# Three 256-column matmuls per group and one VectorE product in the channel-major projections of a two-layer decoder trunk

## The chip, the core and the metric

The kernel runs on one core of one Trainium2 chip. The metric is the device time of one execution in microseconds (us); less is better. A measurement of this kernel is given as the median of its runs. Engines are named as the profile names them: PE is the TensorE matmul, PEld its weight load (which overlaps PE), DVE is VectorE, ACT is ScalarE, POOL is GpSimd, SP is SyncE.

## The reference, cut to what matters

The reference is a causal decoder trunk of two layers over 256 tokens of width 2048 in float32. Each layer normalises its input, multiplies it by wide input weights, mixes over the tokens, projects back and adds the residual; then comes a gated feed-forward part with a causal convolution of width 3 over the tokens.

```python
def rmsnorm(x, g):
    y = xf * lax.rsqrt(jnp.mean(xf * xf, axis=-1, keepdims=True) + NORM_EPS)
    return y * g
...
proj = xn @ w_in                 # even layer: q, k, v, o, gates, u, z
...
def conv_ffn(xn, w_up, conv_w, conv_b, w_down):
    h = xn @ w_up                # 2048 -> 11264
    h = causal_depthwise_conv(h, conv_w) + conv_b
    a, b = jnp.split(h, 2, axis=-1)
    return (jax.nn.silu(a) * b) @ w_down
...
for layer in range(DEPTH):
    h = h + mixer(rmsnorm(h, mix_norm[layer]), ...)
    h = h + conv_ffn(rmsnorm(h, ffn_norm[layer]), ...)
```

The part of the rmsnorm that is one number per token (the reciprocal root) commutes with the matmul, so the kernel applies it to the product. That number is called the token factor here.

## The kernel before, in words

All matmuls run on values that are split in two: hi is the float32 value rounded to the matmul's own float32r type, lo is the rest. A product of two split values is the sum of three matmuls, hi by hi, hi by lo and lo by hi. The activations lie channel-major in four tiles `xc0` to `xc3`, each `[128, 4, 2, 256]`: 128 channels on the partitions, 4 k-tiles, the hi part and the lo part, and 256 tokens. The hi and the lo part of a k-tile stand side by side, 512 columns.

There are two kinds of projection.

- **Token-major** (`tok_plan` with `mm3`, L174 to L178). The activations (128 tokens) are held in the array as the stationary operand, and the weights move through it, 512 columns at most. The three products are three matmuls in a row that add into the same columns. This kind serves v, o, z, the odd layer's input, the output projections and the down projections. One of its steps (L436, the last 256 columns of o, even `w_in` columns 3584 to 3839) is only 256 columns wide, another (L363) 264.
- **Channel-major** (`ch_proj`, L150 to L164). The weights (128 channels) are held, and the tokens move. It serves q and k of the even layer (8 projections of 256 channels), u (4) and the two halves of the up projection (88). A projection has 16 k-tiles and 2 channel tiles `ct`, so 32 groups. A group has one matmul of hi weights by hi and lo activations at once (512 columns, L162, or L159 for the first k-tile) and one of lo weights by hi activations (256 columns, L160), which adds into the second half of the 512 columns. So each accumulator `ps[ct]` ends with two halves that are still to be summed.

`ch_sum` (L166 to L172) does that for each channel tile: ACT copies the second half to `csum` (L170), DVE adds the first half to it (L171), and POOL multiplies by the token factor `rbc`, which is broadcast over the partitions (L172). `rbc` is made once for each normalised input, by the job that ends with L241 (a PE matmul) and L245 (an ACT copy). In the feed-forward `conv_tile` (L828) puts the result behind two zero columns and makes the convolution with one ACT operation (L833) and two DVE operations (L835, L837).

Weights come by DMA on SP's queue, 1 MB at a time (`load_w`, L87). ACT makes hi and DVE makes lo, 1024 columns at a time (both shown at L64), into four buffers each; in a channel-major projection such a buffer holds 4 k-tiles, and a projection uses four of them. Accumulators come from a pool of four PSUM tiles. Each engine runs its instructions in the order in which the program issues them, so a copy for hi stands behind whatever ACT was given before it. Work that doesn't belong to the projections (the normalisation, the mLSTM heads, the attention) is cut into jobs, and `pump` issues a piece of each between the steps.

Of the kernel before, what the change touches and what calls it, by code (L numbers as in the profile page):

```python
# [11 lines left out]
F32 = mybir.dt.float32  # L12
F32R = mybir.dt.float32r
AF = mybir.ActivationFunctionType
ALU = mybir.AluOpType
AX = mybir.AxisListType

P = 128
D = 2048
S = 256  # L20
NT = S // P
KT = D // P
# [18 lines left out]
class Trunk:  # L41
# [107 lines left out]

    def ch_proj(self, w, c0, evac):  # L150
        nc = self.nc
        ps = [self.mm.tile([P, 2, S], F32, tag="mm", name="mm") for _ in range(2)]
        for k0 in range(0, KT, 8):
            for kt, whi, wlo in self.load_w(w, k0, 8, c0, 2 * P):
                x = self.x_both(kt)
                for ct in range(2):
                    c = slice(ct * P, (ct + 1) * P)
                    if kt == 0:
                        nc.tensor.matmul(ps[ct], whi[:, c], x, start=True, stop=False)  # L159
                    nc.tensor.matmul(ps[ct][:, 1], wlo[:, c], x[:, 0], start=False, stop=False)  # L160
                    if kt > 0:
                        nc.tensor.matmul(ps[ct], whi[:, c], x, start=False, stop=kt == KT - 1)  # L162
            self.pump()
        evac(ps)  # L164

    def ch_sum(self, pool, dst, ps):  # L166
        nc = self.nc
        t = pool.tile([P, S], F32, tag="csum", name="csum", bufs=2)
        self.ensure("rbc")
        nc.scalar.copy(t, ps[:, 1])  # L170
        nc.vector.tensor_tensor(t, ps[:, 0], t, op=ALU.add)  # L171
        nc.gpsimd.tensor_tensor(dst, t, self.rbc, op=ALU.mult)  # L172

    def mm3(self, ps, ah, al, bh, bl, start=True, stop=True):  # L174
        nc = self.nc
# [159 lines left out]
    def even(self):  # L335
        nc, I, tc = self.nc, self.I, self.tc
        w_in, w_out = I["even_w_in"][0], I["even_w_out"][0]
        self.yh, self.yl = self.new_y(self.acts, 4)
        with tc.tile_pool(name="ev", bufs=1) as ev, tc.tile_pool(name="ev2", bufs=2) as ev2:
# [100 lines left out]
            for hd in range(4):  # L440
                qk = []
                for j in range(2):
                    dst = ev2.tile([P, 2, S], F32, tag="qk", name="qk", bufs=4)

                    def evac_qk(ps):
                        for ct in range(2):
                            self.ch_sum(ev2, dst[:, ct], ps[ct])
                    self.ch_proj(w_in, j * 1024 + hd * 256, evac_qk)
                    qk.append(dst)
                self.ensure("gates")  # L450
                self.start(self.mlstm_head(hd, ev2, qk, mask, mrow, acol, floor, v1, sig[hd]))

            gu = []
            for g in range(4):
                dst = ev2.tile([P, 2, S], F32, tag="sg", name="gu", bufs=4)

                def evac_u(ps):
                    for ct in range(2):
                        self.ch_sum(ev2, dst[:, ct], ps[ct])
                    nc.scalar.activation(dst, dst, AF.Gelu_apprx_tanh)  # L460
                self.ch_proj(w_in, 4104 + g * 256, evac_u)
                gu.append(dst)
# [355 lines left out]
    def ffn(self, l, gcol, final):  # L818
        nc, I, tc = self.nc, self.I, self.tc
        w_up, w_down = I["ffn_w_up"][l], I["ffn_w_down"][l]  # L820
        conv = self.conv[l]
        with tc.tile_pool(name=f"ff{l}", bufs=1) as ff, tc.tile_pool(name=f"fg{l}", bufs=3) as fg:
            hp = [ff.tile([P, S + 2], F32, name=f"hp{i}") for i in range(4)]
            for t in hp:
                nc.gpsimd.memset(t[:, :2], 0.0)
            turn = [0]

            def conv_tile(ps, cc, name):  # L828
                b = hp[turn[0] % 4]
                turn[0] += 1  # L830
                self.ch_sum(fg, b[:, 2:], ps)
                y = fg.tile([P, S], F32, tag=name, name=name)
                nc.scalar.activation(y, b[:, 2:], AF.Identity, bias=conv[:, 3, cc:cc + 1],  # L833
                                     scale=conv[:, 2, cc:cc + 1])
                nc.vector.scalar_tensor_tensor(y, b[:, 1:S + 1], conv[:, 1, cc:cc + 1], y,  # L835
                                               op0=ALU.mult, op1=ALU.add)
                nc.vector.scalar_tensor_tensor(y, b[:, :S], conv[:, 0, cc:cc + 1], y,  # L837
                                               op0=ALU.mult, op1=ALU.add)
                return y

            base = 0
            for part, nk in enumerate((24, 20)):
                yh, yl = self.new_y(self.acts, 4)
                eh, el = self.new_y(ff, (nk - 16) // 4, 4)
                self.yh, self.yl = yh + eh, yl + el
                for j in range(0, nk, 2):
                    sa = []

                    def evac_a(ps):
                        for ct in range(2):  # L850
                            y = conv_tile(ps[ct], base + j + ct, "ya")
                            nc.scalar.activation(y, y, AF.Silu)
                            sa.append(y)

                    def evac_b(ps):
                        for ct in range(2):
                            y = conv_tile(ps[ct], 44 + base + j + ct, "yb")
                            nc.vector.tensor_tensor(y, sa[ct], y, op=ALU.mult)
                            kt = j + ct
                            self.split(self.yh[kt // 4][:, kt % 4], self.yl[kt // 4][:, kt % 4], y)  # L860
                            self.ready.add(("y", kt))

                    self.ch_proj(w_up, (base + j) * P, evac_a)
                    self.ch_proj(w_up, FFN + (base + j) * P, evac_b)
                last = part == 1
                if last and not final:
                    self.new_xT()
                self.tok_plan(w_down, self.y_at, nk, self.out_steps(nk, base, 0),
                              self.resid(gcol if last else None, final=final and last))
                base += nk  # L870
# [37 lines left out]
```

## Time and profile before

| what | before |
|---|---|
| median of 3 runs | 2192.96 us (2192.69 to 2193.66) |
| span of the profiled execution | 2191.0 us |
| instructions | 28922 |
| PE busy | 2181.2 us, 100%, 11356 matmuls |
| PEld busy | 1858.3 us, 85%, 11356 loads |
| DVE busy | 1418.1 us, 65% |
| ACT busy | 1167.5 us, 53% |
| POOL busy | 177.7 us, 8% |
| HBM | 183 GB/s over the span |

The span runs from the first to the last instruction of the profiled execution; the page gives no other time for that execution, and the runs' times, which hold what lies around the span, are some 2 us longer. Matmuls are pipelined: one starts while the one before is still going through the array, and their ends are modelled. So a busy PE tells little, and the distance from start to start, which the timeline and the chain of waits show, tells how fast it goes. The chain of waits ("chain that ended last") is followed back from the last instruction, at each step to what released it.

### The profile page before, as it was taken

To read this page: it belongs to the slowest core of one execution; us is meant where nothing else is said; L and a number is where in the kernel's file an instruction comes from. 1 tells how busy PE (TensorE), PEld (TensorE's weight loads), DVE (VectorE), ACT (ScalarE), POOL (GpSimd) and SP (SyncE) were. 2 spreads that over 40 slices of the span, in tenths; PEclk is the share of its full clock that TensorE was granted. 3 is DMA by queue.
4 is the path that set the end of the run, shared out by engine and by line. 5 is a ranking of instruction groups with operands and counts; after the bars stand their busy time and mean duration, and the time that the engine had idled before them with its cause. 6 is when DMAs were issued, how large, how long until landed. Compare 5 with 4: busy or idle time off the path is not lost.

```text
span 2191.0 us, 28922 instructions
## 1 busy us (share of the span) xinstructions
PE 2181.2 (100%) x11356; PEld 1858.3 (85%) x11356; DVE 1418.1 (65%) x1991; ACT 1167.5 (53%) x1749; POOL 177.7 (8%) x253
## 2 busy tenths in 40 slices
PE   9999999999999999999999999999999999999999
PEld 7888888888888888888889888888888888888887
DVE  5455565677775457776556887567777644777754
ACT  6544555556564345655445566556655533666632
POOL 0011110111110001111000001001111000111100
PEclk9999999999999999999999999999999999999999
DMA  8555555555555555555556444455555555555563
GB/s 279 182 174 167 178 182 193 176 190 187 181 191 192 192 192 185 183 190 192 184 157 209 154 154 152 160 186 180 186 192 187 189 191 189 186 191 180 187 212 115
DMA packets 310660, 402.51 MB, mean 184 GB/s; under 512 B 7132, under 2 KB 224764, under 8 KB 310524
## 3 DMA queue, kind: packets, MB, share of 16 engines
q1 hardware_dynamic: 309100, 398.44, 55.2%
q10 hardware_dynamic: 1424, 2.23, 0.3%
q8 instruction: 89, 1.46, 0.3%
q14 instruction: 47, 0.39, 0.0%
HBM read 398.54 MB, written 2.10 MB: 183 GB/s over the span
## 4 chain that ended last, share of the span: by engine, by line
PE 94%; issue 4%; DVE 1%; DMA 0%; POOL 0%; ACT 0%; SPq 0%; DVEq 0%; POOLq 0%; ACTq 0%
PE mm L162 32%; PE mm L160 17%; PE mm L178 13%; PE mm L176 13%; PE mm L177 13%; PE mm L159 2%; PE tr L217 1%; PE sm L784 1%; DVE lo L64 0%; PE tr L803 0%; DMA raw<-in_even_w_in 0%; PE sm L486 0%; DVE acc L731 0%; DVE acc L740 0%; PE sm L558 0%
## 5 line engine op out<-in xcount | busy, mean ns | idle before, releaser
L64 DVE TENSOR_TENSOR lo<-raw,hi 128x1024 fp32r<-128x1024 f32 (+3 forms) x764 | 970.4, 1271 | 644.5 <-ACT hi L64 634.7
L64 ACT CAST hi<-raw 128x1024 fp32r<-128x1024 f32 (+3 forms) x764 | 793.1, 1039 | 692.3 <-PE mm L177 412.0
L162 PE MATMUL mm<-xc,hi 128*128 128x512 f32 x3000 | 1062.7, 398 | 0.0
L160 PE MATMUL mm<-xc,lo 128*128 128x256 f32 x3200 | 882.4, 281 | 0.0
L162 PEld LDWEIGHTS mm<-xc,hi 128*128 128x128 f32 x3000 | 563.5, 188 | 133.6
L160 PEld LDWEIGHTS mm<-xc,lo 128*128 128x128 f32 x3200 | 604.0, 189 | 8.8
L176 PE MATMUL mm<-hi,yh 128*128 128x512 f32 x960 | 376.7, 392 | 0.0
L178 PE MATMUL mm<-lo,yh 128*128 128x512 f32 x960 | 375.5, 391 | 0.0
L177 PE MATMUL mm<-hi,yl 128*128 128x512 f32 x960 | 375.1, 391 | 0.0
L172 POOL TENSOR_TENSOR hp<-csum,rbc 128x256 f32<-128x256 f32 x176 | 128.1, 748 | 1128.0 <-DVE csum L171 1105.8
L178 PEld LDWEIGHTS mm<-lo,yh 128*128 128x128 f32 x960 | 180.2, 188 | 38.9
L177 PEld LDWEIGHTS mm<-hi,yl 128*128 128x128 f32 x960 | 180.3, 188 | 38.2
L176 PEld LDWEIGHTS mm<-hi,yh 128*128 128x128 f32 x960 | 180.2, 188 | 37.8
L176 PE MATMUL mm<-hi,xc 128*128 128x512 f32 (+3 forms) x512 | 190.0, 371 | 0.8 <-ACT xc L64 0.8
L178 PE MATMUL mm<-lo,xc 128*128 128x512 f32 (+3 forms) x512 | 189.5, 370 | 0.0
L177 PE MATMUL mm<-hi,xc 128*128 128x512 f32 (+3 forms) x512 | 188.7, 368 | 0.0
L170 ACT COPY csum<-mm 128x256 f32<-128x256 f32 x200 | 72.7, 372 | 139.6 <-PE mm L162 139.6
L171 DVE TENSOR_TENSOR csum<-mm,csum 128x256 f32<-128x256 f32 x200 | 77.9, 424 | 53.9 <-ACT csum L170 53.9
L176 PEld LDWEIGHTS mm<-hi,xc 128*128 128x128 f32 x512 | 96.8, 189 | 14.4 <-ACT xc L64 1.2
L178 PEld LDWEIGHTS mm<-lo,xc 128*128 128x128 f32 x512 | 96.7, 189 | 13.6
L177 PEld LDWEIGHTS mm<-hi,xc 128*128 128x128 f32 x512 | 96.8, 189 | 13.0
L159 PE MATMUL mm<-xc,hi 128*128 128x512 f32 x200 | 74.4, 396 | 0.0
(210 smaller groups left out, 1045.8 us busy)
## 6 DMA issues: line engine op xcount, KB each, us to landing
raw<-in_ffn_w_up SPq DMA_DIRECT2D x176, 1024.0 KB
raw<-in_ffn_w_down SPq DMA_DIRECT2D x88, 1024.0 KB
raw<-in_even_w_in SPq DMA_DIRECT2D x44, 1024.0 KB
raw<-in_odd_w_in SPq DMA_DIRECT2D x24, 1024.0 KB
raw<-in_even_w_out SPq DMA_DIRECT2D x16, 1024.0 KB
raw<-in_odd_w_out SPq DMA_DIRECT2D x16, 1024.0 KB
raw<-in_odd_w_in SPq DMA_DIRECT2D x12, 736.0 KB
out<-h ACTq DMA_DIRECT2D x7, 256.0 KB
```

The costliest lines, as they stand in the source:

```text
L64: ins = call(*args, **kw).ins
L159: nc.tensor.matmul(ps[ct], whi[:, c], x, start=True, stop=False)
L160: nc.tensor.matmul(ps[ct][:, 1], wlo[:, c], x[:, 0], start=False, stop=False)
L162: nc.tensor.matmul(ps[ct], whi[:, c], x, start=False, stop=kt == KT - 1)
L170: nc.scalar.copy(t, ps[:, 1])
L171: nc.vector.tensor_tensor(t, ps[:, 0], t, op=ALU.add)
L172: nc.gpsimd.tensor_tensor(dst, t, self.rbc, op=ALU.mult)
L176: nc.tensor.matmul(ps, ah, bh, start=start, stop=False)
L177: nc.tensor.matmul(ps, al, bh, start=False, stop=False)
L178: return nc.tensor.matmul(ps, ah, bl, start=False, stop=stop)
L217: nc.tensor.transpose(tp[:, tt * P:(tt + 1) * P], self.h[:, tt, kt * P:(kt + 1) * P], self.ident)
L784: nc.tensor.matmul(sp[:, j, :ns], qT[:, 2 * pr + j], kT[:, g, :ns], start=True, stop=True)
```

## The change

The 512-column matmul of a group becomes two of 256 columns, hi weights by hi activations and hi weights by lo activations, and the third, lo weights by hi activations, follows them. All three add into one set of 256 columns, so the accumulator is 256 columns wide and holds the finished sum. `ch_sum` becomes `ch_scale`: one DVE product of the accumulator with `rbc`, straight into the destination. The ACT copy, the DVE sum, the POOL product and the tile `csum` go. The three callers pass the destination alone.

```diff
     def ch_proj(self, w, c0, evac):
         nc = self.nc
-        ps = [self.mm.tile([P, 2, S], F32, tag="mm", name="mm") for _ in range(2)]
+        ps = [self.mm.tile([P, S], F32, tag="mm", name="mm") for _ in range(2)]
         for k0 in range(0, KT, 8):
             for kt, whi, wlo in self.load_w(w, k0, 8, c0, 2 * P):
                 x = self.x_both(kt)
                 for ct in range(2):
                     c = slice(ct * P, (ct + 1) * P)
-                    if kt == 0:
-                        nc.tensor.matmul(ps[ct], whi[:, c], x, start=True, stop=False)
-                    nc.tensor.matmul(ps[ct][:, 1], wlo[:, c], x[:, 0], start=False, stop=False)
-                    if kt > 0:
-                        nc.tensor.matmul(ps[ct], whi[:, c], x, start=False, stop=kt == KT - 1)
+                    nc.tensor.matmul(ps[ct], whi[:, c], x[:, 0], start=kt == 0, stop=False)
+                    nc.tensor.matmul(ps[ct], whi[:, c], x[:, 1], start=False, stop=False)
+                    nc.tensor.matmul(ps[ct], wlo[:, c], x[:, 0], start=False, stop=kt == KT - 1)
             self.pump()
         evac(ps)
 
-    def ch_sum(self, pool, dst, ps):
-        nc = self.nc
-        t = pool.tile([P, S], F32, tag="csum", name="csum", bufs=2)
+    def ch_scale(self, dst, ps):
         self.ensure("rbc")
-        nc.scalar.copy(t, ps[:, 1])
-        nc.vector.tensor_tensor(t, ps[:, 0], t, op=ALU.add)
-        nc.gpsimd.tensor_tensor(dst, t, self.rbc, op=ALU.mult)
+        self.nc.vector.tensor_tensor(dst, ps, self.rbc, op=ALU.mult)
...
-                self.ch_sum(fg, b[:, 2:], ps)
+                self.ch_scale(b[:, 2:], ps)
```

The order on PE, at the start of a projection in the first feed-forward part, is shown with buffer numbers: `mm_...` is the accumulator of a channel tile, `xc0` the first activation tile, `hi` and `lo` the weight buffers. Before:

```order
L159 MATMUL mm_5239<-xc0_2685,hi_5243 128x512
L160 MATMUL mm_5239<-xc0_2685,lo_5244 128x256
L159 MATMUL mm_5240<-xc0_2685,hi_5243 128x512
L160 MATMUL mm_5240<-xc0_2685,lo_5244 128x256
L160 MATMUL mm_5239<-xc0_2685,lo_5244 128x256
L162 MATMUL mm_5239<-xc0_2685,hi_5243 128x512
L160 MATMUL mm_5240<-xc0_2685,lo_5244 128x256
L162 MATMUL mm_5240<-xc0_2685,hi_5243 128x512
```

and in the changed kernel, at the start of such a projection:

```order
L158 MATMUL mm_5863<-xc0_2997,hi_5867 128x256
L159 MATMUL mm_5863<-xc0_2997,hi_5867 128x256
L160 MATMUL mm_5863<-xc0_2997,lo_5868 128x256
L158 MATMUL mm_5864<-xc0_2997,hi_5867 128x256
L159 MATMUL mm_5864<-xc0_2997,hi_5867 128x256
L160 MATMUL mm_5864<-xc0_2997,lo_5868 128x256
```

Each group has three matmuls where it had two, hi before lo in all of them, and no matmul there stands next to one of another width any more.

The order on DVE, at the end of a projection of the first half `ya` in the feed-forward, before (`lo` is a weight split, `hp` the result behind its zero columns):

```order
L64 TENSOR_TENSOR lo<-raw,hi 128x1024 x2
L171 TENSOR_TENSOR csum<-mm,csum 128x256 x2
L64 TENSOR_TENSOR lo<-raw,hi 128x1024
L835 SCALAR_TENSOR_TENSOR ya<-hp_3386,conv_101,ya 128x256
L835 SCALAR_TENSOR_TENSOR ya<-hp_3387,conv_101,ya 128x256
```

and in the changed kernel:

```order
L64 TENSOR_TENSOR lo<-raw,hi 128x1024 x2
L166 TENSOR_TENSOR hp_3698<-mm,rbc 128x256
L166 TENSOR_TENSOR hp_3699<-mm,rbc 128x256
L64 TENSOR_TENSOR lo<-raw,hi 128x1024
L829 SCALAR_TENSOR_TENSOR ya<-hp_3698,conv_101,ya 128x256
```

The two DVE operations keep their place between the same weight splits; they now read `rbc` and write the destination.

## Rows read from the trace of the kernel before

**Rows 1.** The page: busy time of the engines; the chain by engine and by line.

```profile
PE 2181.2 (100%) x11356; PEld 1858.3 (85%) x11356; DVE 1418.1 (65%) x1991; ACT 1167.5 (53%) x1749; POOL 177.7 (8%) x253
...
PE 94%; issue 4%; DVE 1%; DMA 0%; POOL 0%; ACT 0%; SPq 0%; DVEq 0%; POOLq 0%; ACTq 0%
PE mm L162 32%; PE mm L160 17%; PE mm L178 13%; PE mm L176 13%; PE mm L177 13%; PE mm L159 2%; PE tr L217 1%; PE sm L784 1%; DVE lo L64 0%; PE tr L803 0%; DMA raw<-in_even_w_in 0%; PE sm L486 0%; DVE acc L731 0%; DVE acc L740 0%; PE sm L558 0%
```

**Rows 2.** Waits of PE, longest first: us in total, times, longest us.

```profile
PE tr L264 <- DMA rows<-in_mix_norm: 3.3, 1, 3.3
...
PE mm L176 <- ACT xc L64: 0.8, 1, 0.8
```

**Rows 3.** Windows: 264-column and 256-column token-major stretches, then the up projection.

```profile
core 0: us, PE busy (x) PEld busy (x) DVE busy (x) ACT busy (x) POOL busy (x), PEclk, DMA share, GB/s
34.50:42.00 7.50, 7.50 (x61) 7.34 (x61) 3.55 (x6) 4.90 (x11) 0.71 (x1) 1.00 1.00 323
49.00:53.80 4.80, 4.80 (x43) 4.80 (x42) 3.87 (x4) 1.41 (x2) 0.00 (x0) 1.00 0.56 179
800.00:1000.00 200.00, 200.00 (x1136) 173.73 (x1135) 144.06 (x205) 118.32 (x173) 24.43 (x34) 1.00 0.57 186
```

**Rows 4.** Chain, 800 to 1000 us: start us, us, what; first and last "x2".

```profile
809.14 0.24 PE mm L160 x2
...
989.73 0.24 PE mm L160 x2
```

**Rows 5.** Timeline of PE in the up projection: start us, us, engine, line, operation.

```profile
900.10 0.28 PE L160 MATMUL mm<-xc,lo 128*128 128x256 f32 x1
900.22 0.39 PE L162 MATMUL mm<-xc,hi 128*128 128x512 f32 x1
900.44 0.28 PE L160 MATMUL mm<-xc,lo 128*128 128x256 f32 x1
...
902.21 0.28 PE L160 MATMUL mm<-xc,lo 128*128 128x256 f32 x1
```

**Rows 6.** Timeline of PE in the token-major step of 256 columns: first and last.

```profile
56.23 0.28 PE L178 MATMUL mm<-lo,xc 128*128 128x256 f32 x1
...
59.95 0.28 PE L176 MATMUL mm<-hi,xc 128*128 128x256 f32 x1
```

**Rows 7.** Timeline of PE in a token-major step of 512 columns: first and last.

```profile
83.81 0.39 PE L177 MATMUL mm<-hi,xc 128*128 128x512 f32 x1
...
85.85 0.39 PE L177 MATMUL mm<-hi,xc 128*128 128x512 f32 x1
```

**Rows 8.** Groups of the page: xcount | busy us, mean ns | idle before, releaser.

```profile
L172 POOL TENSOR_TENSOR hp<-csum,rbc 128x256 f32<-128x256 f32 x176 | 128.1, 748 | 1128.0 <-DVE csum L171 1105.8
...
L170 ACT COPY csum<-mm 128x256 f32<-128x256 f32 x200 | 72.7, 372 | 139.6 <-PE mm L162 139.6
L171 DVE TENSOR_TENSOR csum<-mm,csum 128x256 f32<-128x256 f32 x200 | 77.9, 424 | 53.9 <-ACT csum L170 53.9
```

**Rows 9.** Waits of all engines: ACT's hi split for PE in the projections.

```profile
ACT hi L64 <- PE mm L162: 239.5, 241, 2.0
```

**Rows 10.** Timelines of ACT, then DVE, 404 to 413 us, first feed-forward part.

```profile
407.64 0.38 ACT L245 COPY rbc<-tr 128x256 f32<-128x256 f32 x1
...
406.48 0.77 DVE L171 TENSOR_TENSOR csum<-mm,csum 128x256 f32<-128x256 f32 x2 [1.18 <-ACT csum L170]
407.78 1.23 DVE L64 TENSOR_TENSOR lo<-raw,hi 128x1024 fp32r<-128x1024 f32 x1 [0.52 <-ACT hi L64]
```

**Rows 11.** Timeline of PE at the start of a projection.

```profile
910.56 0.40 PE L160 MATMUL mm<-xc,lo 128*128 128x256 f32 x2
910.79 0.40 PE L162 MATMUL mm<-xc,hi 128*128 128x512 f32 x1
```

**Rows 12.** Timeline of PE in the token-major step of 264 columns: first and last.

```profile
36.08 0.28 PE L177 MATMUL mm<-hi,xc 128*128 128x264 f32 x1
...
37.90 0.28 PE L177 MATMUL mm<-hi,xc 128*128 128x264 f32 x1
```

More of the change, by code (lines that the diff above doesn't have):

```diff
@@ L446, in evac_qk @@
                         for ct in range(2):
-                            self.ch_sum(ev2, dst[:, ct], ps[ct])
+                            self.ch_scale(dst[:, ct], ps[ct])
                     self.ch_proj(w_in, j * 1024 + hd * 256, evac_qk)
@@ L458, in evac_u @@
                     for ct in range(2):
-                        self.ch_sum(ev2, dst[:, ct], ps[ct])
+                        self.ch_scale(dst[:, ct], ps[ct])
                     nc.scalar.activation(dst, dst, AF.Gelu_apprx_tanh)
```

## The prediction

> **What bounds the kernel now.** I read the page first: TensorE (PE) is busy for 2181.2 us of a span of 2191.0 us and it makes 94% of the chain that ended last; one matmul goes with one weight load, 11356 of each [rows 1]. The three lines of the channel-major projection are 32%, 17% and 2% of that chain, about half of the kernel. The waits of PE come next: the longest is 3.3 us, at the start, and no line of the projection is among them [rows 2]. So PE's instruction stream, not a neighbour, sets the time, and what counts is how far apart matmuls start. Their busy times don't tell that (a 512-column matmul is "busy" 398 ns, yet they start far closer), so I read starts. The windows show the clock granted in full in every stretch, the upper of its two levels, 2.4 GHz, and 16% of the weight loader's time free in the projection: 173.73 of 200 us busy [rows 3].
>
> **The pace before.** Each projection begins with one "L160 x2" row in the chain of waits (the one place where two 256-column matmuls follow each other). From 809.14 to 989.73 us there are 17 such rows, 16 periods: 11.287 us a projection [rows 4]. A projection has 16 k-tiles by 2 channel tiles, 32 groups of one 256- and one 512-column matmul, so a group takes 352.7 ns. The timeline agrees: six groups from 900.10 to 902.21, 352 ns each; the 512-column matmul starts 0.12 us after the 256-column one, the next 256-column one 0.22 us after that [rows 5]. There are 100 projections (44 in each feed-forward layer, 8 for q and k, 4 for u), 3200 groups.
>
> **What the change does on PE.** A group becomes three 256-column matmuls: the same 768 columns, one matmul and one weight load more, 3200 of each in all. What does a 256-column matmul cost in a stream of its own kind? The trace has such a stream: the token-major step at line 436 (even w_in columns 3584 to 3839), where hi, lo and hi products of 256 columns follow each other and add into one set of columns, as the changed group will. There they start exactly 0.12 us apart, 31 intervals from 56.23 to 59.95 us [rows 6]. Three make 360 ns. I take this value, because width, number of weight loads and accumulation are those of the changed kernel; only what is held and what moves are exchanged (weights move there, the activations will here).
>
> It is a fair price for other reasons too. Token-major 512-column matmuls start 226.7 ns apart (9 intervals, 83.81 to 85.85) [rows 7]. Between 256 and 512 columns lie 106.7 ns, 0.417 ns a column, and that leaves 13.3 ns a matmul whatever its width. A 512-column stream spreads these 13.3 ns over twice the columns; the changed kernel spreads them over 256. The present mixed group doesn't reach the sum of its parts (226.7 + 120 = 346.7), it takes 6 ns more, and this excess is what makes the change cheaper than a full 13.3 ns.
>
> Term 1: (360 - 352.7) ns x 3200 = **+23.3 us**, all of it on the path, since PE waits for nobody.
>
> Bounds for the group. Below: columns alone, 768 x 0.417 = 320 ns, -104.6 us. Above: the present 352.7 ns plus one more whole fixed price, 366.0 ns, +42.7 us. The row that has three such matmuls says 360, so I take that.
>
> The Trainium skill (TensorE: Matmul & The Clock Gate, "Back-to-back issue gap") puts the gap at columns over clock plus about 2.5 ns. By it a third matmul in the group costs 2.5 ns, and the sum would be +8 us, 2201 us. The trace agrees on the 0.417 ns a column and not on the fixed part, which is 13.3 ns here, with one weight load per matmul.
>
> **The evacuation.** Removed: 200 ACT copies (L170, 372 ns, 72.7 us) and 200 POOL products (L172; the 176 of the feed-forward take 748 ns, 128.1 us); the 200 DVE sums of 424 ns (L171) become 200 DVE products of the same size, also with one operand in PSUM [rows 8]. DVE's own work stays equal, so 0 there; bounded by the row it can hardly differ by more than its 424 ns each. All of it runs beside PE: no PE wait names any of these lines [rows 2]. Value on the path: 0. Nor does it help that mm's columns come free earlier: four accumulators exist, a projection takes two, and PE never waits for one. The cover is PE's own 11.3 us per projection; if it were gone, a projection would gain or lose the chain's length, about 1 us.
>
> Term 2: 0. ACT and DVE have slack for the weight splits: ACT waits 239.5 us, 241 times, for PE to free a hi buffer in these stages [rows 9], so splits run ahead of PE until the four buffers are full.
>
> **A new wait.** The DVE product needs rbc, the old DVE sum didn't (POOL did). At the first projection of a feed-forward, DVE summed at 406.48, its next weight split began at 407.78, and rbc was written by ACT from 407.64 to 408.02 [rows 10]. DVE will stand until rbc is there, and the split queued behind it, and the feed of PE through it, come up to some 1.1 us later (less, as ACT is rid of two copies ahead of rbc). Four buffers of 4 k-tiles, 2.8 us of PE work each, cover that: 0. Without the cover it is two times 1.1, +2 us. DMA issues don't move; the loads wait for the same splits.
>
> **Sum.** The profiled span is 2191.0 us and the median of the runs 2192.96, 2 us around it that the change leaves alone. 2192.96 + 23.3 + 0 = **2216 us**, +1.06%. A measurement of this kernel can tell about 0.2%, 4.4 us, from no change.
>
> **Rivals.**
> 1. *No change.* 256-column matmuls inside the projection go at 117.5 ns, not 120: there, the two that follow each other take 0.23 us together until the next 512-column one starts [rows 11]. Three at 117.5 are 352.5 ns: -0.2 x 3200 = -0.6 us, 2192 us. For it: that row is from the very stage. Against: each is next to a 512-column matmul, and the one long steady stream shows 120. Within the bound at 117.1 to 118.0 ns a matmul. Chance 0.16.
> 2. *Between the two*, with a pace of 118.5 ns: +2.8 x 3200 = +9 us, 2202 us. It is what a small fixed price would do, as in the Trainium skill's section named above. The token-major stream of 264 columns speaks for it a little: 15 intervals in 1.82 us, 121.3 ns, hardly more than 256 columns need, so the fixed price isn't a strict 13.3 ns [rows 12]. Chance 0.08.
> 3. *The whole fixed price is added* and the projection's 6 ns of excess stay: 366.0 ns, +42.7 us, 2236 us. For it: the excess could belong to this stage's operands rather than to mixed widths. Against: the 256-column stream has none. Chance 0.08.
> 4. *Faster: the second load of the same weights is dropped.* The first two matmuls of a group hold the same whi slice. If the second needed no load, and so not its 13.3 ns, a group would take 346.7 ns: -6.0 x 3200 = -19.2 us, 2174 us. It decides from 351.3 ns a group downward. Against: the page has one load for each matmul in every group, 11356 and 11356, but it holds no two neighbours with equal weights, so it can't exclude it. Chance 0.08.
> 5. *The loader or the feeding falls behind.* In the 256-column stretch the weight loader is busy 4.80 of 4.80 us, against 87% in the projection now [rows 3]; there is no room left in it. If it slips by 3 ns a load, that is +29 us more, some 2245 us; were the late rbc uncovered, 2 us more. Against: at a DMA share of 1.00 in the 264-column stretch [rows 3] the pace held. Chance 0.04.
>
> **How the numbers follow.** The forecast has 0.56; its own range is 2209 to 2224 us (119.3 to 120.8 ns a matmul). With the case between (2202) and no change (2189 to 2197) that is 0.80, so the range is 2189 to 2228; left out are 2174, 2236 and 2245. Slower by over 0.2%: 0.56 + 0.08 + 0.08 + 0.03 = 0.75. Within 0.2%: 0.16 + 0.01 = 0.17. Faster: 0.08.
>
> **What would show it.** Right: in the feed-forward the periods of the projection are 11.52 us in place of 11.287; matmuls of its three lines start 0.12 us apart; the loader is busy for nearly all of the time in these windows; PE's waits are as short as before; ACT and POOL lose their lines and the time doesn't notice; token-major stages keep 226.7 ns. The extra matmuls are 3200, and so are the loads. Wrong: a period of 11.28 us (rival 1) or 11.71 us (rival 3), fewer loads than matmuls (rival 4), or a PE wait on DVE's lo in the projection (rival 5).

## The result and the profile after

The changed kernel takes 2217.88 us (median of 4 runs, 2217.08 to 2218.63), the kernel before beside it 2192.88 us (2192.69 to 2193.66). The ratio is 1.0115, 95% interval 1.0103 to 1.0128: slower by 25.0 us, where 2216 us, 23 us more, had been forecast. The profiled span grew from 2191.0 to 2215.4 us.

The page of the changed kernel, with the lines that answer to [rows 1] and [rows 8] (L158, L159 and L160 are now the three matmuls of a group, L166 the DVE product, L827 the ACT step of the convolution):

```profile
PE 2205.3 (100%) x14556; PEld 2029.9 (92%) x14556; DVE 1378.8 (62%) x1991; ACT 1082.2 (49%) x1549; POOL 33.2 (1%) x53
...
PE mm L159 17%; PE mm L158 17%; PE mm L160 17%; PE mm L172 13%; PE mm L171 13%; PE mm L170 13%; PE tr L211 1%; PE sm L778 1%; DVE lo L64 0%; DMA raw<-in_even_w_in 0%; PE tr L797 0%; PE sm L480 0%; DVE acc L725 0%; DVE acc L734 0%; PE sm L552 0%
...
L160 PE MATMUL mm<-xc,lo 128*128 128x256 f32 x3200 | 905.6, 283 | 0.0
...
L160 PEld LDWEIGHTS mm<-xc,lo 128*128 128x128 f32 x3200 | 614.2, 192 | 0.0
...
L166 DVE TENSOR_TENSOR hp<-mm,rbc 128x256 f32<-128x256 f32 x176 | 69.0, 425 | 24.6 <-PE mm L160 24.6
```

Matmuls and loads each went from 11356 to 14556, 3200 more, and each group of matmuls still has as many loads. DVE, ACT and POOL have less to do, POOL nearly nothing; the span is longer all the same. The DVE product takes 425 ns, as the DVE sum did [rows 8].

PE's timeline in the up projection of the changed kernel, start and duration in us, answers to [rows 5]:

```profile
919.74 0.28 PE L158 MATMUL mm<-xc,hi 128*128 128x256 f32 x1
919.86 0.28 PE L159 MATMUL mm<-xc,hi 128*128 128x256 f32 x1
919.98 0.28 PE L160 MATMUL mm<-xc,lo 128*128 128x256 f32 x1
920.10 0.28 PE L158 MATMUL mm<-xc,hi 128*128 128x256 f32 x1
...
921.90 0.28 PE L158 MATMUL mm<-xc,hi 128*128 128x256 f32 x1
```

18 intervals in 2.16 us: 0.12 us each, 360 ns a group, the pace of the token-major stream of the kernel before [rows 6]. The steady projections of the feed-forward start 11.52 us apart (at 1002.18, 1013.70 and 1025.22 us, for instance) where they started 11.287 us apart before [rows 4]. The window from 900 to 1000 us of the changed kernel and PE's waits say the rest (columns as in [rows 3] and [rows 2]):

```profile
900.00:1000.00 100.00, 100.00 (x835) 100.00 (x835) 69.39 (x107) 51.08 (x71) 0.00 (x0) 1.00 0.56 180
```

```profile
PE tr L258 <- DMA rows<-in_mix_norm: 3.4, 1, 3.4
PE mm L170 <- ACT xc L64: 1.6, 1, 1.6
```

PE runs 835 matmuls in 100 us, the weight loader is busy all the time (87% before), the granted clock is 1.00, still the upper level, and no wait of a projection has appeared. PE waits for nothing new; it has more to issue.

### The profile page after: what moved, and what is told of

Read it like the earlier page. It is cut to its first block, busy times and chain, and to the rows that moved or that the text cites. A ratio compares the mean times of both kernels' runs of the same rounds, so it can differ in the third digit from the quotient of the medians.

```text
span 2215.4 us, 35109 instructions
## 1 busy us (share of the span) xinstructions
PE 2205.3 (100%) x14556; PEld 2029.9 (92%) x14556; DVE 1378.8 (62%) x1991; ACT 1082.2 (49%) x1549; POOL 33.2 (1%) x53
## 4 chain that ended last, share of the span: by engine, by line
PE 94%; issue 4%; DVE 1%; DMA 0%; POOL 0%; ACT 0%; SPq 0%; DVEq 0%; POOLq 0%
PE mm L159 17%; PE mm L158 17%; PE mm L160 17%; PE mm L172 13%; PE mm L171 13%; PE mm L170 13%; PE tr L211 1%; PE sm L778 1%; DVE lo L64 0%; DMA raw<-in_even_w_in 0%; PE tr L797 0%; PE sm L480 0%; DVE acc L725 0%; DVE acc L734 0%; PE sm L552 0%
## 5 line engine op out<-in xcount | busy, mean ns | idle before, releaser
L64 DVE TENSOR_TENSOR lo<-raw,hi 128x1024 fp32r<-128x1024 f32 (+3 forms) x764 | 923.9, 1210 | 734.7 <-ACT hi L64 718.1
L64 ACT CAST hi<-raw 128x1024 fp32r<-128x1024 f32 (+3 forms) x764 | 792.0, 1037 | 1008.7 <-PE mm L159 476.4
L158 PE MATMUL mm<-xc,hi 128*128 128x256 f32 x3200 | 906.6, 284 | 0.0
L159 PE MATMUL mm<-xc,hi 128*128 128x256 f32 x3200 | 905.6, 283 | 0.0
L160 PE MATMUL mm<-xc,lo 128*128 128x256 f32 x3200 | 905.6, 283 | 0.0
L159 PEld LDWEIGHTS mm<-xc,hi 128*128 128x128 f32 x3200 | 614.3, 192 | 0.7 <-DVE xc L64 0.4
L158 PEld LDWEIGHTS mm<-xc,hi 128*128 128x128 f32 x3200 | 614.0, 192 | 0.3
L160 PEld LDWEIGHTS mm<-xc,lo 128*128 128x128 f32 x3200 | 614.2, 192 | 0.0
L166 DVE TENSOR_TENSOR hp<-mm,rbc 128x256 f32<-128x256 f32 x176 | 69.0, 425 | 24.6 <-PE mm L160 24.6
L827 ACT ACTIVATE ya<-hp,conv 128x256 f32<-128x256 f32 x88 | 48.1, 594 | 2.7 <-DVE hp L166 2.7
```

The source lines that it names most:

```text
L64: ins = call(*args, **kw).ins
L158: nc.tensor.matmul(ps[ct], whi[:, c], x[:, 0], start=kt == 0, stop=False)
L159: nc.tensor.matmul(ps[ct], whi[:, c], x[:, 1], start=False, stop=False)
L160: nc.tensor.matmul(ps[ct], wlo[:, c], x[:, 0], start=False, stop=kt == KT - 1)
L166: self.nc.vector.tensor_tensor(dst, ps, self.rbc, op=ALU.mult)
```

## The experiments

Two theories went in with the forecast's numbers: all of the loss is the pace of the matmuls, and 120 ns is 106.7 ns of columns plus a fixed 13.3 ns. The rivals were a share of the evacuation in the loss, a pace that belongs to the stage's operands, and a pace that the weight loader sets. Each ratio is to the kernel before on the same chip.

### One part of the change at a time

The run mm_only has the changed matmuls with a long evacuation. Against the changed kernel (the lines that make the tile `csum` and the callers are left out):

```diff
-        self.nc.vector.tensor_tensor(dst, ps, self.rbc, op=ALU.mult)
+        nc.scalar.copy(t, ps)
+        nc.vector.tensor_tensor(t, ps, t, op=ALU.max)
+        nc.gpsimd.tensor_tensor(dst, t, self.rbc, op=ALU.mult)
```

> The changed matmuls (three of 256 columns a group) with an evacuation of three steps like the one before: ACT copies the accumulator to csum, DVE takes the maximum of accumulator and copy (they are equal), POOL multiplies by the token factor. Theory (all of the loss is the matmuls' pace, 120 ns each): 2217 to 2218 us, ratio 1.0115 to the kernel before. Rival (part of the loss, the 1 to 2 us over the forecast, comes from the DVE product that waits for rbc, or the evacuation gave something back): 2 us or more off 2217.9.

Measured: 2218.42 us, ratio 1.0115 (1.0102 to 1.0129). The whole loss is there with the evacuation undone. The stretches of its projections agree with the changed kernel's to 0.01 us: 103.55 us from the first matmul of q to the last of k, 640.16 us from the first to the last of the first feed-forward part.

The run evac_only has the matmuls of before with the short evacuation. Against the kernel before:

```diff
-        nc = self.nc
-        t = pool.tile([P, S], F32, tag="csum", name="csum", bufs=2)
         self.ensure("rbc")
-        nc.scalar.copy(t, ps[:, 1])
-        nc.vector.tensor_tensor(t, ps[:, 0], t, op=ALU.add)
-        nc.gpsimd.tensor_tensor(dst, t, self.rbc, op=ALU.mult)
+        self.nc.vector.tensor_tensor(dst, ps[:, 0], self.rbc, op=ALU.mult)
```

> The matmuls of the kernel before (512 and 256 columns a group) with an evacuation of one DVE product of the first half of the accumulator by the token factor; it leaves out the second half, that is the hi by lo and lo by hi products, in the sum. ACT copy, DVE sum and POOL product are gone. Theory (the evacuation is hidden behind PE): 2193 us, within 0.1% of the kernel before. Rival (the shorter evacuation frees engines that PE waits for): faster by 2 us or more; rival (the DVE product stands for rbc and delays the splits): slower by 1 to 2 us.

Measured: 2193.01 us against 2192.62, ratio 1.0000 (0.9991 to 1.0009). Its page shows ACT, DVE and POOL as short of work as in the changed kernel, to no effect:

```profile
PE 2181.9 (100%) x11356; PEld 1859.0 (85%) x11356; DVE 1376.7 (63%) x1991; ACT 1083.0 (49%) x1549; POOL 31.5 (1%) x53
```

So the evacuation is worth 0 within some 2 us (0.09%), and the matmuls are all of it.

### Why the mixed group took 352.7 ns and not 346.7

The forecast rested on the mixed group being 6 ns dearer than its parts. The run eq384 has two matmuls of equal width in a group, with the 768 columns and the two loads of the kernel before. Its edit, against the changed kernel (the accumulator of 384 columns and the product of its first 256 are left out):

```diff
-                    nc.tensor.matmul(ps[ct], whi[:, c], x[:, 0], start=kt == 0, stop=False)
-                    nc.tensor.matmul(ps[ct], whi[:, c], x[:, 1], start=False, stop=False)
-                    nc.tensor.matmul(ps[ct], wlo[:, c], x[:, 0], start=False, stop=kt == KT - 1)
+                    xf = x.rearrange("p a s -> p (a s)")[:, :384]
+                    nc.tensor.matmul(ps[ct], whi[:, c], xf, start=kt == 0, stop=False)
+                    nc.tensor.matmul(ps[ct], wlo[:, c], xf, start=False, stop=kt == KT - 1)
```

> A group of two matmuls of 384 columns, hi weights and lo weights by the hi activations of all tokens and the lo activations of the first 128: the 768 columns and two loads of the kernel before, but of equal width. It leaves out hi weights by lo activations for 128 tokens and adds lo by lo for the others; the evacuation is one DVE product of the first 256 columns. Theory (a matmul costs columns at 0.417 ns and 13.3 ns, the excess is the changing width): 346.7 ns a group, 2173 to 2174 us. Rival (the operands of the stage): 352.7 ns, 2193 us.

Measured: 2175.85 us, ratio 0.9923 (0.9910 to 0.9937), 17.0 us less than before, 5.3 ns a group. PE's timeline of this run:

```profile
919.71 0.33 PE L159 MATMUL mm<-xc,hi 128*128 128x384 f32 x1
919.88 0.33 PE L160 MATMUL mm<-xc,lo 128*128 128x384 f32 x1
...
921.79 0.33 PE L159 MATMUL mm<-xc,hi 128*128 128x384 f32 x1
```

12 intervals in 2.08 us, 173.3 ns: 160 ns of columns and 13.3 ns. So the operands of the stage cost nothing extra, and the unequal neighbours are left as the cause. The run grouped4 tests them with the matmuls of the kernel before: it computes the same product and puts equal neighbours together, four k-tiles at a time (the lines taken out and those that set `c` are not shown):

```diff
+            for i in range(0, 8, 4):
+                group = [(kt, whi, wlo, self.x_both(kt)) for kt, whi, wlo in parts[i:i + 4]]
+                for kt, whi, wlo, x in group:
+                    for ct in range(2):
+                        nc.tensor.matmul(ps[ct], whi[:, c], x, start=kt == 0, stop=False)
+                for kt, whi, wlo, x in group:
+                    for ct in range(2):
+                        nc.tensor.matmul(ps[ct][:, 1], wlo[:, c], x[:, 0], start=False,
+                                         stop=kt == KT - 1)
```

> The kernel before, with the matmuls of four k-tiles put in another order: eight of 512 columns (hi weights), then eight of 256 (lo weights), so that neighbours have equal width. Theory (a matmul costs its columns and a fixed 13.3 ns, and the 6 ns a group beyond that come from alternating widths): a group at 226.7 + 120 = 346.7 ns in place of 352.7, 19 us less, 2174 us. Rival (the excess belongs to the operands of this stage, weights held and tokens moving): 235 ns for the 512 and 117.5 for the 256, 2193 us, no change. Rival (hi first makes PE wait for lo or the order costs buffers): slower.

Measured: 2182.49 us, ratio 0.9953 (0.9940 to 0.9965): half of what was expected, 10.1 us or 3.2 ns a group. The chain of waits shows where the other half is (start, us, what):

```profile
916.09 0.95 PE mm L164 x8
917.04 1.84 PE mm L160 x8
918.88 0.95 PE mm L164 x8
919.84 1.84 PE mm L160 x8
```

Eight of 256 columns take 0.95 us, 119 ns each, but eight of 512 take 1.84 us, 230 ns, not 226.7. So a change of width is paid for over some matmuls. The run snake8 changes the width less often (cut as before):

```diff
+            for which in ("hi", "lo") if k0 == 0 else ("lo", "hi"):
+                for kt, whi, wlo, x in parts:
+                    for ct in range(2):
+                        if which == "hi":
+                            nc.tensor.matmul(ps[ct], whi[:, c], x, start=kt == 0, stop=kt == KT - 1)
+                        else:
+                            nc.tensor.matmul(ps[ct][:, 1], wlo[:, c], x[:, 0], start=False, stop=False)
```

> The kernel before with its matmuls ordered by eight k-tiles, hi weights (512 columns) then lo weights (256 columns) in the first half of a projection, lo then hi in the second, so that a projection changes width twice in place of eight times as in the run grouped4. Theory (the 6 ns a group are paid after a change of width and die away over some matmuls: in grouped4 a change to 512 and back cost 19 ns over the 346.7 ns a group of equal neighbours): one such pair of changes a projection in place of four, 58 ns a projection less than grouped4, 6 us in all, 2176 to 2177 us. Rival (the rest of the excess belongs to the operands of this stage): 2182 us as grouped4. Rival (PE waits for lo or for buffers, which are held for eight k-tiles): slower than grouped4, with PE waits on DVE's lo or ACT's hi in the projections.

Measured: 2177.16 us, ratio 0.9930 (0.9916 to 0.9943), as expected. It is a full version of the kernel with the evacuation of before, 15.7 us faster than the kernel before and 41 us faster than the changed one. Its chain:

```profile
907.06 3.83 PE mm L163 x32
910.90 7.28 PE mm L161 x32
918.18 3.83 PE mm L163 x32
922.01 7.28 PE mm L161 x32
```

A projection is 32 of 512 columns in 7.28 us (227.5 ns each) and 32 of 256 in 3.83 us (119.7 ns), 347 ns a group, against 352.7 before and 360 in the changed kernel. PE's longest wait stayed at 3.3 us; holding eight k-tiles at a time cost nothing. Smaller windows of the same chain show where the price of a change lies, at the start of one run of 32 matmuls of 512 columns and from its sixth on:

```profile
910.90 0.93 PE mm L161 x4
...
912.06 5.89 PE mm L161 x26
```

The first four take 232 ns each, the 26 from the sixth on 226.5. The five behind the change take 1.16 us together (910.90 to 912.06), some 27 ns more than five at 226.7; where the width falls again, the first 256-column matmul takes 113 ns and not 120, which gives back some 7. In the runs of eight of grouped4 the first four take 0.93 us too. So the price, some 20 ns, is paid once for each pair of changes, whether 8 or 32 matmuls follow.

### What the 120 ns are

The run split128 cuts one of the three matmuls of a group in two.

> The changed kernel with the lo by hi matmul cut into two of 128 columns, so four matmuls and four loads a group. Theory (120 ns is 106.7 ns of columns and 13.3 ns fixed): two of 128 columns take 66.7 ns each, a group 373.3 ns, 43 us more than the changed kernel, 2261 us. Rival (the 120 ns are the weight loader's, which needs 108 to 120 ns a load whatever moves behind it): two of 128 columns take 216 to 240 ns, a group 456 to 480 ns, 307 to 384 us more, 2525 to 2602 us.

Its edit:

```diff
-                    nc.tensor.matmul(ps[ct], wlo[:, c], x[:, 0], start=False, stop=kt == KT - 1)
+                    nc.tensor.matmul(ps[ct][:, :P], wlo[:, c], x[:, 0, :P], start=False, stop=False)
+                    nc.tensor.matmul(ps[ct][:, P:], wlo[:, c], x[:, 0, P:], start=False, stop=kt == KT - 1)
```

Measured: 2547.43 us, ratio 1.162 (1.160 to 1.164), 329.5 us over the changed kernel. The theory's 43 us is far off; the rival's 307 to 384 us holds it. PE and the loader in this run, one group and the start of the next:

```profile
1000.16 0.33 PE L158 MATMUL mm<-xc,hi 128*128 128x256 f32 x1
1000.33 0.28 PE L159 MATMUL mm<-xc,hi 128*128 128x256 f32 x1
1000.45 0.22 PE L160 MATMUL mm<-xc,lo 128*128 128x128 f32 x1
1000.51 0.28 PE L161 MATMUL mm<-xc,lo 128*128 128x128 f32 x1
1000.63 0.33 PE L158 MATMUL mm<-xc,hi 128*128 128x256 f32 x1
```

```profile
1000.10 0.19 PEld L158 LDWEIGHTS mm<-xc,hi 128*128 128x128 f32 x1
1000.21 0.19 PEld L159 LDWEIGHTS mm<-xc,hi 128*128 128x128 f32 x1
1000.33 0.19 PEld L160 LDWEIGHTS mm<-xc,lo 128*128 128x128 f32 x1
1000.45 0.19 PEld L161 LDWEIGHTS mm<-xc,lo 128*128 128x128 f32 x1
1000.57 0.19 PEld L158 LDWEIGHTS mm<-xc,hi 128*128 128x128 f32 x1
```

The matmuls start unevenly, 0.17, 0.12, 0.06 and 0.12 us apart; the loads start evenly, 0.11 to 0.12 us apart, whatever moves. Four loads make the group of 0.47 us, 116 ns a load: with matmuls this narrow among the others the loader sets the pace. The run w192 asks whether it also does at 256 columns:

```diff
-                    nc.tensor.matmul(ps[ct], whi[:, c], x[:, 0], start=kt == 0, stop=False)
+                    nc.tensor.matmul(ps[ct], whi[:, c], x[:, 0, :192], start=kt == 0, stop=False)
```

(and the same for the other two; the narrower accumulator and the second DVE product are left out)

> The changed kernel with 192 of the 256 columns in each of the three matmuls (the last 64 tokens of the projections are left out and filled from other tokens by a second DVE product). Theory (120 ns is 106.7 ns of columns and 13.3 ns fixed): 93.3 ns a matmul, 280 ns a group, 256 us less than the changed kernel, 1962 us. Rival (the weight loader sets the pace, 116 ns a load as in the run split128, up to 120): 348 to 360 ns a group, 2179 to 2218 us. In between: loader at the 108 ns of the 128-column transposes, 324 ns a group, 2103 us.

Measured: 2138.60 us, ratio 0.975 (0.974 to 0.977), 79.3 us under the changed kernel where columns alone would give 256 us. In the chain of this run nine groups take 3.02 us, 111.9 ns a matmul:

```profile
919.91 0.11 PE mm L158
...
922.93 0.11 PE mm L158
```

None of the three numbers on record was met, but they bracket it: 93.3 ns is out, and a load and matmul take 112 ns here, between the 108 and 116 ns that had been put down for the loader. The Trainium skill (TensorE: Matmul & The Clock Gate, "LDWEIGHTS (loading the stationary operand)") gives the time of a load in ns as its columns divided by 1.2, by estimate 107 ns for 128 columns. The 112 ns of w192 lie 5 ns above that, the 116 ns of split128 9 ns.

What makes up the 120 ns at 256 columns stays open. They lie on the line of columns plus 13.3 ns on which 384 and 512 columns lie (173.3 and 226.7 ns). But the kernel before has a stream of 264 columns that lies under this line: 121.3 ns [rows 12], where columns plus 13.3 ns would be 123.3. From 192 to 256 columns a matmul grows by 8 ns and from 256 to 264 by 1.3, 0.13 and 0.16 ns a column; from 384 to 512 it grows by 53.4, 0.417 a column. So the loader may have a part in the pace at 256 columns too, and no run separates the two.

### A repeated load

The run interleave changes the order in the group, so that no two neighbours hold the same weights.

```diff
                     nc.tensor.matmul(ps[ct], whi[:, c], x[:, 0], start=kt == 0, stop=False)
-                    nc.tensor.matmul(ps[ct], whi[:, c], x[:, 1], start=False, stop=False)
-                    nc.tensor.matmul(ps[ct], wlo[:, c], x[:, 0], start=False, stop=kt == KT - 1)
+                    nc.tensor.matmul(ps[ct], wlo[:, c], x[:, 0], start=False, stop=False)
+                    nc.tensor.matmul(ps[ct], whi[:, c], x[:, 1], start=False, stop=kt == KT - 1)
```

> The changed kernel with the order hi, lo, hi in each group in place of hi, hi, lo, so that no two neighbours hold the same weights (except across nothing). Theory (a repeated load costs what any load costs): 2217 to 2218 us as the changed kernel. Rival (a repeated load is cheaper, or dearer): another time by 3 us or more.

Measured: 2218.28 us, ratio 1.0117 (1.0104 to 1.0131), the changed kernel's time. In both orders there are 14556 loads for 14556 matmuls: weights that the matmul before held are loaded again, at the full price.

## Why the prediction was right

**The term.** Three matmuls at 120 ns, taken from the only stream of 256-column matmuls in the trace [rows 6], gave 360 ns a group, and the changed kernel shows 360 ns. 23.3 us were forecast, 25.0 measured (22.6 to 28.1 by the interval). The rest lies on PE where matmuls of the jobs stand between the groups. In the even layer PE went from 149.4 us (106.02 to 255.39, first matmul of q to last of u) to 153.5 us (105.43 to 258.88), 1.3 us more than twelve projections at 0.233. The two feed-forward parts gained 10.7 us each from their first to their last projection, 0.4 more than 44 projections at 0.233. Together the projections gained 25.4 us in the profiled executions, and the span gained 24.4. What the jobs do to the groups isn't shown.

**The base.** The group of before was taken as measured, 352.7 ns [rows 4], and not as a sum of parts. That was needed: the sum of parts (346.7) would have given 43 us. The working called the 6 ns between them an excess of the mixed group. eq384 and snake8 show that it is one, and that nearly all of it (5.3 and 4.9 ns a group) goes when neighbours have equal width.

**The evacuation.** Term 2 was 0, and evac_only measures 0.0% (-0.09 to 0.09%), for the reason given: PE's waits don't name it before or after.

**The new wait** didn't come as told. DVE was said to stand for rbc ahead of a weight split. The timelines of ACT and DVE in the changed kernel show another order:

```profile
410.72 0.37 ACT L239 COPY rbc<-tr 128x256 f32<-128x256 f32 x1
...
410.85 1.23 DVE L64 TENSOR_TENSOR lo<-raw,hi 128x1024 fp32r<-128x1024 f32 x1 [2.11 <-ACT hi L64]
411.99 0.75 DVE L166 TENSOR_TENSOR hp<-mm,rbc 128x256 f32<-128x256 f32 x2
```

At this first projection of a feed-forward part the split stands ahead of the products, where it stood behind the DVE sum before [rows 10]. rbc is written at 411.09, before DVE is done with the split, so DVE never stood for it. The wait had been priced at 0, for a cover that was not called on; the sum wasn't touched.

**The rivals.** The pace of 117.5 ns seen beside 512-column matmuls [rows 11] belongs to the mixed stream: matmuls of 256 columns among their own kind run at 120 ns in this stage too. No load was dropped, and the loader, busy all the time, didn't fall behind. Its busy share says little about how near it was to that: in eq384 it is also busy for 100.00 of 100 us, at one load in 173 ns, since a load is shown as some 190 ns long. The rule of the Trainium skill named in the prediction (TensorE: Matmul & The Clock Gate, "Back-to-back issue gap") is given there for the gap of an isolated matmul, and would have made 2201 us. With a load for each matmul, the rows here show 13.3 ns over the columns at 256, 384 and 512 columns, not 2.5.

**What was too simple.** The working took 13.3 ns a matmul "whatever its width", from two widths. At 192 columns that would give 93.3 ns where 111.9 were measured, and at 264 columns the working's own row shows 121.3 where it would give 123.3. The forecast stood on a row of the right width, so this didn't matter. Two readings were off, without a part in the sum: the loader's free time in the projection was 13% (26.27 of 200 us) and not 16%, and the next 256-column matmul mostly starts 0.23 to 0.24 us after the 512-column one; 0.22, beside the 0.12, would make a group of 340 ns.

## What to carry to other kernels

Price a cut of matmuls by a row of the trace that has the new width among equal neighbours, start to start: each matmul brings its weight load and a price beyond its columns with it, and shorter vector work beside a PE that waits for nobody gives nothing back. Where matmuls of two widths alternate, ordering them so that equal widths follow each other can be worth more than the edit at hand: here it took 0.7% off the kernel without a change in the work. Below some 256 columns a matmul with its own weight load hardly gets cheaper: 192 columns took 112 ns where 256 took 120, and the loads of split128 kept 116 ns apart.

## What the runs showed of the hardware that was not expected

A change of width between neighbouring matmuls costs time: some 6 ns a group where 512 and 256 columns alternate, and some 20 ns for each pair of changes where runs are long, paid by the first five 512-column matmuls. What in the engine does it stays open; no run here separates the load that is issued during a narrow matmul from other causes.

DVE's weight splits (L64), 1271 ns on average before, took 1210 ns in evac_only, with the matmuls unchanged and POOL's products and ACT's copies gone:

```profile
L64 DVE TENSOR_TENSOR lo<-raw,hi 128x1024 fp32r<-128x1024 f32 (+3 forms) x764 | 923.5, 1210 | 730.2 <-ACT hi L64 715.8
```

The changed kernel and the four other runs without POOL's products and ACT's copies have 1209 to 1211 ns, and mm_only, grouped4 and snake8, which have both, 1226 to 1230. So the splits take longer with that work around; which of the two does it, and why the kernel before has the longest, no run separates. It moved no time, as PE doesn't wait for them.
